# Narrow triangular products and quarters of a dense projection in alternation on TensorE

## The chip, the core and the metric

The kernel runs on one core of a Trainium2 chip. The metric is the device time of one execution in microseconds (us), as the median of several runs. TensorE (PE) multiplies matrices; a product is a weight load (PEld) and a pass of moving columns. VectorE (DVE), ScalarE (ACT) and GpSimd (POOL) do the elementwise work, and SyncE (SP) issues most transfers.

## The reference, cut to what matters

Four layers act on 512 tokens of width 1024: two of a first kind (attention and long convolution) and two of a second kind. The change is in the second kind alone, so it acts twice in an execution. Such a layer holds a gated delta rule (four heads, 128 wide), a latent attention and a gated linear recurrence:

```python
# gated delta rule: a unit triangular system for every chunk and head
a_mat = where(strict, einsum(kbeta, kc) * decay, 0.0) + eye(C)
sol = triangular_solve(a_mat, rhs, lower=True, unit_diagonal=True)
u, w = sol[..., :DV], sol[..., DV:]
_, o = lax.scan(step, state0, xs)          # the state runs over the chunks
o_a = rmsnorm(o, gdn_out_norm) * silu(gz)
...
# linear recurrence
u = causal_dwconv(lx, lru_conv_w) + lru_conv_b
o_c = rg_lru(u, ...) * silu(lz)            # lz = 512 columns of h @ w_in
mixed = concatenate([o_a, o_b, o_c])
return x + mixed @ w_out
```

## The kernel before

Everything is written in Tile, which takes the instructions in the order of the code and gives each engine its own queue in an order that it plans by modelled times: an instruction whose inputs or buffers are not there is passed over, and a later one that is ready is put ahead of it. On the chip each queue then runs in that order. `issue_after(ins)`, used through `self.after`, makes the matmuls traced inside it stand behind `ins` in TensorE's queue.

A dense projection (`projT`) takes one chunk of weights of 128 by 1024 and 24 matmuls of 512 moving columns, three for each of eight blocks of the contraction, since each factor is held as a rounded part and a remainder (`wh`, `wl`). `wchunk` fetches a chunk (line 280), ACT rounds it (line 266), DVE or POOL makes the remainder (line 267). There are two raw buffers (`wr`) and three each of `wh` and `wl`, shared by all projections and taken in the order of the code.

A layer of the second kind (`layer2`) traces, in this order: `mla_pre`; `gdn_front`, which builds the triangular blocks and solves their 32-wide diagonal blocks on DVE (`solve32`, a chain of 62 operations), sends the result to DRAM (line 1396) and fetches it back spread over the partitions (`spread`, lines 1415 and 1417); `lru_open`, three convolution projections; `gdn`, which first has four gate projections for `gz`, then the inverse (`gdn_inv`), then the state recurrence of four steps; `lru`, the linear recurrence in four column blocks c; `mla_v` and `mla`, the attention.

`gdn_inv` joins the 32-wide inverses to 128-wide ones by four sets of narrow products, `p1` (line 1440), `p2` (1446 and 1448), `p3` (1459) and `p4` (1464). Each set has four steps i, each step four heads, and each head one float32 product (two in `p2`), which the trace counts as two instructions with 128 weight columns and 32 or 64 moving columns. A step writes half of a PSUM buffer; ACT copies it out (lines 1442, 1453, 1455, 1460, 1465), and the later sets read the copies. Then `pw` and `pu` (lines 1470 and 1474, 128 moving columns) apply the inverse.

`lru(c)` runs two products with block weights (lines 1228 and 1231), a chain of ACT, DVE and POOL work to a scan, and then the projection of its output gate (24 matmuls with chunk 28 + c), whose `silu2` (lines 701 and 702) goes to a tile `gz` of its own; POOL multiplies it with the scan into `o`. In c = 2 the fourth convolution projection, `conv(3)`, stands ahead of that block's products.

Of the kernel before, what the change touches and what calls it, by code (L numbers as in the profile page):

```python
# [16 lines left out]
ADD, SUB, MUL, MAX = ALU.add, ALU.subtract, ALU.mult, ALU.max  # L17

P = 128
# [149 lines left out]
class Kern:  # L169
# [672 lines left out]
    def gates(self, l, h, ma, mg):  # L842

        ma.append(self.U())
        mg += [self.U(), self.T("mg", (P, 4, S))]
        for f in range(4, 8):
            self.gate(l, h, 32 + f, ma[1][:, f - 4])
            yield
        for f in range(8):
            self.gate(l, h, 40 + f, mg[f // 4][:, f % 4])  # L850
            yield
# [337 lines left out]
    def lru_open(self, l, h):  # L1189

        nc, A = self.nc, self.A
        c2 = self.c2
        bh = self.sm(8, "bh")
        nc.vector.tensor_scalar(bh, c2[:, C2_BR:C2_BR + 8], 0.5, None, op0=MUL)
        sp = self.sm(4, "sp")
        nc.vector.tensor_scalar(sp, c2[:, C2_AP:C2_AP + 4], -1.0, None, op0=MUL)
        sp = self.softplus(sp, 4)
        sp2, ny = self.sm(4, "sp2"), self.sm(4, "ny")
        nc.vector.tensor_scalar(sp2, sp, 2.0, None, op0=MUL)
        nc.vector.tensor_scalar(ny, sp, -4.0, None, op0=MUL)  # L1200
        us = {}

        def conv(c):
            ps = self.ps("acc")
            last = self.projT(self.wchunk(A[f"xin{l}"][24 + c], 8, P), h, ps)
            us[c] = self.T("g2" if c == 2 else "lu")
            self.conv4(us[c], ps, C2_LW + 4 * c, bias=c2[:, C2_LB + c:C2_LB + c + 1])
            return last

        for c in range(3):  # L1210
            last = conv(c)
        return bh, sp2, ny, us, conv, last

    def lru(self, l, h, opened):
        nc, A = self.nc, self.A
        bh, sp2, ny, us, conv, _ = opened
        o = self.U()
        for c in range(4):
            w = self.T("lw", (P, 2, P))
            nc.gpsimd.memset(w, 0.0)  # L1220
            for q in range(2):
                r = slice(64 * q, 64 * q + 64)
                nc.sync.dma_start(w[r, :, r], A[f"lw{l}"][q][:, c])
            if c == 2:
                conv(3)
            u = us[c]
            pr, pi = self.ps("av"), self.ps("av")
            nc.tensor.matmul(pr, w[:, 0], u, start=True, stop=True)
            t, ti, dc = self.T("l"), self.T("g2"), self.T("l")
            nc.scalar.activation(t, pr, AF.Tanh, scale=0.5, bias=bh[:, c:c + 1])  # L1230
            nc.tensor.matmul(pi, w[:, 1], u, start=True, stop=True)
            nc.scalar.activation(ti, pi, AF.Tanh, scale=0.5, bias=bh[:, 4 + c:5 + c])
            nc.vector.scalar_tensor_tensor(u, ti, 1.0, u, op0=ADD, op1=MUL)

            nc.scalar.activation(dc, t, AF.Exp, scale=ny[:, c:c + 1], bias=ny[:, c:c + 1])
            nc.scalar.activation(t, t, AF.Tanh, scale=sp2[:, c:c + 1], bias=sp2[:, c:c + 1])
            nc.scalar.activation(t, t, AF.Sqrt, scale=0.25)
            nc.vector.scalar_tensor_tensor(t, dc, 1.0, t, op0=ADD, op1=MUL)
            nc.gpsimd.tensor_tensor(u, u, t, op=MUL)
            nc.vector.tensor_tensor_scan(t, dc, u, 0.0, op0=MUL, op1=ADD)  # L1240
            ps = self.ps("acc")
            self.projT(self.wchunk(A[f"xin{l}"][28 + c], 8, P), h, ps)
            gz = self.T("l")
            self.silu2(gz, ps)
            nc.gpsimd.tensor_tensor(o[:, c], t, gz, op=MUL)
        return o

    def decays(self, l, gab):
# [172 lines left out]
            nc.vector.transpose(self.diag(XT, k), xc[rs(k)])  # L1421
        return xd, xc, xtc, XT

    def gdn_inv(self, lead, at, t1, X, kb, v2):


        nc = self.nc
        mm = nc.tensor.matmul
        cp = nc.scalar.activation
        xd, xc, xtc, XT = X  # L1430

        def banks(tag, shape):
            ps = [self.ps(tag, (P, 2) + shape) for _ in range(2)]
            return [ps[i // 2][:, i % 2] for i in range(4)]

        p1 = banks("lg", (4, 64))
        for i in range(4):
            with self.after(lead):
                for c in range(4):
                    mm(p1[i][:, c], at[:, i, c], xd[:, 4 * i + c], start=True, stop=True)  # L1440
            for b in (0, 64):
                cp(t1[b + 32:b + 64, i, :, b:b + 32], p1[i][b + 32:b + 64, :, b // 2:b // 2 + 32], AF.Copy)
        p2 = banks("tr", (2, 4, 32))
        for i in range(4):
            for c in range(4):
                mm(p2[i][:, 0, c], XT[:, i, c], t1[:, i, c, 0:32], start=True, stop=True)
            for c in range(4):
                mm(p2[i][:, 1, c], t1[:, i, c], xtc[:, 4 * i + c], start=True, stop=True)

            xi = xd[:, 4 * i:4 * i + 4]  # L1450
            nc.gpsimd.memset(xi[64:96, :, 32:64], 0.0)
            nc.gpsimd.tensor_copy(xi[32:64, :, 32:64], xc[32:64, 4 * i:4 * i + 4])
            cp(xi[32:64, :, 0:32], p2[i][32:64, 0], AF.Copy, scale=-1.0)
            for b in (0, 64):
                cp(XT[b:b + 32, i, :, b + 32:b + 64], p2[i][b:b + 32, 1], AF.Copy, scale=-1.0)
        p3 = banks("lg", (4, 64))
        for i in range(4):
            for c in range(4):
                mm(p3[i][:, c], at[:, i, c], xd[:, 4 * i + c], start=True, stop=True)
            cp(t1[64:128, i, :, 0:64], p3[i][64:128], AF.Copy)  # L1460
        p4 = banks("tr", (4, 64))
        for i in range(4):
            for c in range(4):
                mm(p4[i][:, c], t1[:, i, c], XT[:, i, c, 64:128], start=True, stop=True)
            cp(XT[0:64, i, :, 64:128], p4[i][0:64], AF.Copy, scale=-1.0)
        for i in range(4):
            ts = slice(i * P, (i + 1) * P)
            pw = self.ps("lg", (P, 4, P))
            for c in range(4):
                mm(pw[:, c], kb[:, i, c], XT[:, i, c], start=True, stop=True)  # L1470
            cp(kb[:, i], pw, AF.Copy)
            pu = self.ps("tr", (P, 4, P))
            for c in range(4):
                mm(pu[:, c], XT[:, i, c], v2[:, c, ts], start=True, stop=True)
            cp(v2[:, :, ts], pu, AF.Copy)

    def gdn(self, l, h, lead, q2, k2, v2, at, an, kb, egs, ssq, t1, X):
        nc, A = self.nc, self.A
        mm = nc.tensor.matmul
        gz = self.U()  # L1480
        for c in range(4):
            ps = self.ps("acc")
# [2 lines left out]

        for i in range(4):
            nc.gpsimd.tensor_tensor(at[:, i], at[:, i], self.mbc(self.lv), op=MUL)
        self.gdn_inv(lead, at, t1, X, kb, v2)
        kd, un, wt = k2, v2, kb

        st = [self.T("st", (P, 2, P)) for _ in range(2)]
# [5 lines left out]
        for i in range(4):  # L1497
# [3 lines left out]
            for q in range(2):  # L1501
                hs = slice(2 * q, 2 * q + 2)
                s1 = st[q]
                ps = self.ps("lg", (P, 2, P))
# [15 lines left out]
            o = self.T("go", (P, 4, P))  # L1520
            nc.vector.tensor_tensor(o, po, self.bc(eg[:, 0:4]), op=MUL)
            p2 = self.ps("tr", (P, 4, P))
# [7 lines left out]
            r = self.sm(4, "hr")  # L1530
# [129 lines left out]
```

## Time and profile before

| | us |
|---|---|
| median of three runs | 1890.8 |
| lowest and highest run | 1885.38, 1893.59 |
| profiled execution, its own time | 1893.08 |
| its span in the trace | 1891.3 |
| TensorE busy in the span | 1854.0 (98%) |
| DVE, ACT, POOL busy | 1254.6, 900.1, 659.9 |
| mean granted TensorE clock | 0.992 of full speed |

The span runs from the first to the last instruction, and 1.8 us of the execution's time lie around it. Times below are from the span's start. A matmul's listed duration is that of its passage; matmuls overlap, and what one costs in a row is the distance from its start to the next one's start.

### The profile page before, as it was taken

To read this page: it belongs to the slowest core of one execution; us is meant where nothing else is said; L and a number is where in the kernel's file an instruction comes from. 1 tells how busy PE (TensorE), PEld (TensorE's weight loads), DVE (VectorE), ACT (ScalarE), POOL (GpSimd) and SP (SyncE) were. 2 spreads that over 40 slices of the span, in tenths; PEclk is the share of its full clock that TensorE was granted. 3 is DMA by queue.
4 is the path that set the end of the run, shared out by engine and by line. 5 is a ranking of instruction groups with operands and counts; after the bars stand their busy time and mean duration, and the time that the engine had idled before them with its cause. 6 is when DMAs were issued, how large, how long until landed. Compare 5 with 4: busy or idle time off the path is not lost.

```text
span 1891.3 us, 26054 instructions
## 1 busy us (share of the span) xinstructions
PE 1854.0 (98%) x9604; PEld 1560.9 (83%) x9604; DVE 1254.6 (66%) x2238; ACT 900.1 (48%) x1761; POOL 659.9 (35%) x566
## 2 busy tenths in 40 slices
PE   8999999999999999999999999999999999999998
PEld 5878888887788788888888888888888888888886
DVE  6898688664788849775567954757235895465722
ACT  4766432334476542223455356656325535665631
POOL 2455343443245535443146332111114643311110
PEclk9999999999999999999999989999999998999999
DMA  5333433324323353233332321213343222121242
GB/s 178 98 120 110 145 112 107 112 89 164 116 96 106 105 160 108 100 101 123 128 105 70 97 73 30 69 59 115 101 136 101 79 84 79 36 69 59 77 131 90
DMA packets 75656, 190.84 MB, mean 101 GB/s; under 512 B 15714, under 2 KB 25698, under 8 KB 75528
## 3 DMA queue, kind: packets, MB, share of 16 engines
q1 hardware_dynamic: 69448, 184.71, 30.1%
q0 software_dynamic: 1696, 3.41, 0.7%
q10 hardware_dynamic: 4384, 1.05, 0.3%
q8 instruction: 76, 1.25, 0.3%
q14 instruction: 52, 0.43, 0.1%
HBM read 171.29 MB, written 17.84 MB: 100 GB/s over the span
## 4 chain that ended last, share of the span: by engine, by line
PE 75%; DVE 13%; issue 4%; ACT 3%; POOL 3%; DMA 2%; ACTq 0%; SPq 0%; DVEq 0%; POOLq 0%
PE acc L258 13%; PE acc L260 13%; PE acc L259 13%; PE fl L259 5%; PE fl L258 5%; PE fl L260 5%; PE av L1181 2%; DVE wl L267 2%; DVE g L1005 1%; PE av L259 1%; PE av L258 1%; PE av L260 1%; PE av L588 1%; PE lg L259 1%; PE lg L260 1%
## 5 line engine op out<-in xcount | busy, mean ns | idle before, releaser
L266 ACT ACTIVATE wh<-wr 128x1024 fp32r<-128x1024 f32 (+3 forms) x268 | 256.0, 955 | 448.3 <-PE acc L259 160.9
L258 PE MATMUL acc<-u,wh 128*128 128x512 f32 x996 | 397.1, 399 | 0.2
L259 PE MATMUL acc<-u,wh 128*128 128x512 f32 x996 | 393.2, 395 | 0.0
L260 PE MATMUL acc<-u,wl 128*128 128x512 f32 x996 | 392.5, 394 | 0.0
L267 POOL TENSOR_TENSOR wl<-wr,wh 128x1024 fp32r<-128x1024 f32 (+3 forms) x86 | 186.2, 2165 | 490.1 <-ACT wh L266 451.0
L267 DVE TENSOR_TENSOR wl<-wr,wh 128x1024 fp32r<-128x1024 f32 (+3 forms) x182 | 217.5, 1195 | 170.0 <-ACT wh L266 159.6
L258 PEld LDWEIGHTS acc<-u,wh 128*128 128x128 f32 x996 | 187.2, 188 | 42.7 <-issue 3.7
L260 PEld LDWEIGHTS acc<-u,wl 128*128 128x128 f32 x996 | 187.2, 188 | 39.5 <-issue 2.6
L259 PEld LDWEIGHTS acc<-u,wh 128*128 128x128 f32 x996 | 187.3, 188 | 38.3 <-issue 2.9
L259 PE MATMUL fl<-u,wh 128*128 128x512 f32 x316 | 128.6, 407 | 0.0
L260 PE MATMUL fl<-u,wl 128*128 128x512 f32 x316 | 126.5, 400 | 0.0
L258 PE MATMUL fl<-u,wh 128*128 128x512 f32 x316 | 125.9, 398 | 0.0
L260 PE MATMUL acc<-wh,u 128*128 128x512 f32 (+1 forms) x212 | 79.5, 375 | 0.3
L258 PE MATMUL acc<-wh,u 128*128 128x512 f32 (+1 forms) x212 | 78.2, 376 | 1.6 <-DVE l L702 1.2
L259 PE MATMUL acc<-wl,u 128*128 128x512 f32 (+1 forms) x212 | 78.7, 371 | 0.0
L260 PEld LDWEIGHTS fl<-u,wl 128*128 128x128 f32 x316 | 60.3, 191 | 14.9 <-issue 3.0
L259 PEld LDWEIGHTS fl<-u,wh 128*128 128x128 f32 x316 | 60.3, 191 | 13.3 <-issue 2.0
L258 PEld LDWEIGHTS fl<-u,wh 128*128 128x128 f32 x316 | 60.1, 190 | 13.2 <-issue 1.5
L677 ACT ACTIVATE p<-p,mx 128x512 f32<-128x512 f32 x64 | 45.7, 715 | 37.4 <-DVE mx L675 37.4
L790 POOL TENSOR_TENSOR w<-w,ab 128x256 f32<-128x256 f32 x32 | 37.7, 1179 | 69.2 <-DVE w L789 64.0
L321 ACT ACTIVATE sq<-x 128x512 f32<-128x512 f32 x40 | 25.2, 631 | 68.6 <-DVE x L1613 38.2
L1168 ACT ACTIVATE p<-p,amx 128x128 f32<-128x128 f32 (+1 forms) x64 | 35.8, 560 | 28.2 <-DVE amx L1167 27.5
(636 smaller groups left out, 4438.7 us busy)
## 6 DMA issues: line engine op xcount, KB each, us to landing
wr<-in_win SPq DMA_DIRECT2D x88, 512.0 KB, 3.5
wr<-in_xin SPq DMA_DIRECT2D x64, 512.0 KB, 3.4
wr<-in_xout SPq DMA_DIRECT2D x32, 512.0 KB, 3.5
hd<-f SPq DMA_DIRECT2D x32, 256.0 KB, 4.2
hs<-hd SPq DMA_DIRECT2D x32, 256.0 KB, 2.8
wr<-in_wout SPq DMA_DIRECT2D x16, 512.0 KB, 3.4
xd<-x SPq DMA_DIRECT2D x12, 512.0 KB, 3.1
x<-xd SPq DMA_DIRECT2D x12, 512.0 KB, 4.8
```

The costliest lines, as they stand in the source:

```text
L258: mm(ps, l[0], r[0], start=first, stop=False)
L259: mm(ps, l[0], r[1], start=False, stop=False)
L260: return mm(ps, l[1], r[0], start=False, stop=last)
L266: nc.scalar.activation(hi, src, AF.Copy)
L267: (nc.gpsimd if pool else nc.vector).tensor_tensor(lo, src, hi.bitcast(F32), op=SUB)
L321: self.nc.scalar.activation(self.T("sq"), self.xt(i)[:, h * S:(h + 1) * S], AF.Square, scale=1.0 / math.sqrt(D), accum_out=self.ms2[i][:, ...
L588: nc.tensor.matmul(po[:, i], wt[:, kt], v[:, kt, hd * P:(hd + 1) * P], start=kt == 0, stop=kt == 3)
L677: nc.scalar.activation(pp[c], pp[c], AF.Exp, bias=mx[:, c:c + 1], accum_out=s0[:, i:i + 1] if c == 0 else s)
L790: nc.gpsimd.tensor_tensor(a[:, 0], a[:, 0], b[:, 1], op=ADD)
L1005: nc.vector.scalar_tensor_tensor(y[:, d:], ps[:, :S - d], w(n), y[:, d:], op0=MUL, op1=ADD)
L1168: nc.scalar.activation(p[:, :n], p[:, :n], AF.Exp, bias=mx, scale=scale, accum_out=s)
L1181: mm(po[:, ts], v[hd // 4][:, k, (hd % 4) * P:(hd % 4 + 1) * P], w[:, k], start=k == 0, stop=k == i)
```

## The change

The four output gate projections of the linear recurrence move from `lru` into the inverse. `lru_open` now returns a generator, `gates()`, that traces them in order, with a halt after every second of the eight blocks of the contraction, that is after six matmuls. So there are 16 quarters. `gdn_inv` takes the steps of `p1` to `p4` and the quarters in turn: step, quarter, step, quarter, 16 times; each stands behind the one before in TensorE's queue by `issue_after`. The first step stands behind the third convolution projection, as before. The gate's `silu2` writes to `o[:, c]`, and the scan is multiplied into it in place, so that the separate tile for the gate is gone. `o` is allocated with the first quarter. `pw`, `pu` and the state recurrence are as they were.

```diff
+        def gates():
+            o.append(self.U())
+            for c in range(4):
+                ps = self.ps("acc")
+                hi, lo = self.wchunk(A[f"xin{l}"][28 + c], 8, P)
+                for k in range(8):
+                    last = self.mm3(ps, (hi[:, k], lo[:, k]), h[k], k == 0, k == 7)
+                    if k == 7:
+                        self.silu2(o[0][:, c], ps)
+                    if k % 2:
+                        yield last
...
-        return bh, sp2, ny, us, conv, last
+        return bh, sp2, ny, us, conv, o, (last, gates())
...
-            ps = self.ps("acc")
-            self.projT(self.wchunk(A[f"xin{l}"][28 + c], 8, P), h, ps)
-            gz = self.T("l")
-            self.silu2(gz, ps)
-            nc.gpsimd.tensor_tensor(o[:, c], t, gz, op=MUL)
+            nc.gpsimd.tensor_tensor(o[:, c], t, o[:, c], op=MUL)
...
+        def turn(products):
+            nonlocal last
+            for each in (products, lambda: next(other)):
+                with self.after(last):
+                    last = each()
+
+        def four(p, left, right):
+            for c in range(4):
+                r = mm(p[:, c], left(c), right(c), start=True, stop=True)
+            return r
...
         for i in range(4):
-            with self.after(lead):
-                for c in range(4):
-                    mm(p1[i][:, c], at[:, i, c], xd[:, 4 * i + c], start=True, stop=True)
+            turn(lambda: four(p1[i], lambda c: at[:, i, c], lambda c: xd[:, 4 * i + c]))
...
-            for c in range(4):
-                mm(p2[i][:, 0, c], XT[:, i, c], t1[:, i, c, 0:32], start=True, stop=True)
-            for c in range(4):
-                mm(p2[i][:, 1, c], t1[:, i, c], xtc[:, 4 * i + c], start=True, stop=True)
+            def both():
+                four(p2[i][:, 0], lambda c: XT[:, i, c], lambda c: t1[:, i, c, 0:32])
+                return four(p2[i][:, 1], lambda c: t1[:, i, c], lambda c: xtc[:, 4 * i + c])
+
+            turn(both)
...
-            for c in range(4):
-                mm(p3[i][:, c], at[:, i, c], xd[:, 4 * i + c], start=True, stop=True)
+            turn(lambda: four(p3[i], lambda c: at[:, i, c], lambda c: xd[:, 4 * i + c]))
...
-            for c in range(4):
-                mm(p4[i][:, c], t1[:, i, c], XT[:, i, c, 64:128], start=True, stop=True)
+            turn(lambda: four(p4[i], lambda c: t1[:, i, c], lambda c: XT[:, i, c, 64:128]))
```

## Rows read from the trace of the kernel before

**Rows 1.** The page: busy us (share of the span) and instructions of each engine.

```profile
PE 1854.0 (98%) x9604; PEld 1560.9 (83%) x9604; DVE 1254.6 (66%) x2238; ACT 900.1 (48%) x1761; POOL 659.9 (35%) x566
```

**Rows 2.** TensorE's waits over the span: us in total, times, longest.

```profile
PE ft L349 <- DVE xn L342: 7.5, 1, 7.5
PE lg L667 <- DVE mx L671: 5.1, 3, 2.1
...
PE acc L258 <- DVE l L702: 1.2, 1, 1.2
```

**Rows 3.** Stretches: us, then busy us (instructions) by engine, PEclk, DMA share, GB/s.

```profile
1109.00:1114.50 5.50, 5.50 (x51) 5.46 (x49) 3.61 (x4) 1.88 (x7) 3.45 (x8) 0.99 0.31 75
1114.50:1117.90 3.40, 3.40 (x8) 2.06 (x8) 0.00 (x0) 2.14 (x5) 0.40 (x2) 0.51 0.32 123
1117.90:1121.30 3.40, 3.40 (x33) 3.40 (x31) 0.76 (x2) 3.35 (x6) 0.00 (x0) 0.99 0.00 0
1121.30:1128.10 6.80, 6.80 (x25) 5.48 (x25) 0.98 (x2) 4.25 (x10) 0.32 (x1) 0.50 0.00 0
...
1588.60:1595.50 6.90, 6.90 (x25) 5.50 (x25) 0.14 (x1) 2.96 (x8) 2.23 (x5) 0.52 0.20 78
...
1598.90:1605.70 6.80, 6.80 (x26) 5.48 (x26) 0.99 (x2) 4.23 (x10) 0.32 (x1) 0.51 0.00 0
```

**Rows 4.** TensorE in order of time, third layer: start, us, line, operands, count.

```profile
1092.05 1.02 PE L1228 MATMUL av<-lu,lw 128*128 128x512 f32 x2
...
1098.38 1.02 PE L1231 MATMUL av<-lu,lw 128*128 128x512 f32 x2
...
1102.88 0.39 PE L259 MATMUL acc<-u,wh 128*128 128x512 f32 x1
1103.11 0.39 PE L260 MATMUL acc<-u,wl 128*128 128x512 f32 x1
1103.56 1.97 PE L1440 MATMUL lg<-xd,at 128*128 128x64 f32 x16
...
1109.10 1.90 PE L1440 MATMUL lg<-xd,at 128*128 128x64 f32 x16
1110.83 1.03 PE L1446 MATMUL ft<-X,XT 128*128 128x32 f32 x8
...
1122.37 2.80 PE L1459 MATMUL lg<-xd,at 128*128 128x64 f32 x12
1124.96 2.02 PE L1231 MATMUL av<-lu,lw 128*128 128x512 f32 x2
...
1145.14 1.06 PE L1470 MATMUL lg<-XT,kb 128*128 128x128 f32 x8
1145.96 0.48 PE L258 MATMUL acc<-u,wh 128*128 128x512 f32 x1
1146.27 0.40 PE L259 MATMUL acc<-u,wh 128*128 128x512 f32 x1
```

**Rows 5.** TensorE's groups between 1092 and 1103.5 us, one of three alike.

```profile
L258 PE MATMUL acc<-u,wh 128*128 128x512 f32 x14 | 6.3, 447 | 0.0
```

**Rows 6.** POOL in order of time; in brackets the idle time before, and its releaser.

```profile
1096.90 0.66 POOL L1396 DMA_DIRECT2D dm<-u  x1 [12.18 <-DVE u L1395]
...
1100.21 1.39 POOL L1415 DMA_DIRECT2D xd<-dm  x2 [1.98 <-DMA dm<-u]
```

**Rows 7.** ACT in order of time: roundings of weight chunks, and a copy of `p1`.

```profile
1092.02 1.06 ACT L266 ACTIVATE wh<-wr 128x1024 fp32r<-128x1024 f32 x1 [3.90 <-DVE st L1393]
...
1098.39 1.06 ACT L266 ACTIVATE wh<-wr 128x1024 fp32r<-128x1024 f32 x1 [0.61 <-POOL st L1516]
...
1104.67 0.55 ACT L1442 ACTIVATE X<-lg 32x128 f32<-32x128 f32 x2 [2.73 <-PE lg L1440]
...
1106.78 1.06 ACT L266 ACTIVATE wh<-wr 128x1024 fp32r<-128x1024 f32 x1 [0.66 <-PE acc L259]
```

**Rows 8.** TensorE in order of time, fourth layer.

```profile
1579.66 1.97 PE L1440 MATMUL lg<-xd,at 128*128 128x64 f32 x16
```

More of the change, by code (lines that the diff above doesn't have):

```diff
@@ L1208, in conv @@
             return last
+        o = []
+        def gates():
[9 more added lines that the diff above has]
+                        yield last
         for c in range(3):
             last = conv(c)
-        return bh, sp2, ny, us, conv, last
+        return bh, sp2, ny, us, conv, o, (last, gates())
     def lru(self, l, h, opened):
         nc, A = self.nc, self.A
-        bh, sp2, ny, us, conv, _ = opened
-        o = self.U()
+        bh, sp2, ny, us, conv, (o,), _ = opened
         for c in range(4):
@@ L1422, in spread, with gdn_inv @@
         return xd, xc, xtc, XT
-    def gdn_inv(self, lead, at, t1, X, kb, v2):
+    def gdn_inv(self, last, other, at, t1, X, kb, v2):
         nc = self.nc
@@ L1487, in gdn @@
             nc.gpsimd.tensor_tensor(at[:, i], at[:, i], self.mbc(self.lv), op=MUL)
-        self.gdn_inv(lead, at, t1, X, kb, v2)
+        self.gdn_inv(*lead, at, t1, X, kb, v2)
         kd, un, wt = k2, v2, kb
```

## The prediction

> **What bounds the kernel now.** I read the page first: TensorE is busy for 1854.0 of 1891.3 us, and no other engine comes above 66% [rows 1]. The view of TensorE's waits over the whole span says the same from the other side: the largest is 7.5 us ahead of the first work, then 5.1 us in three parts of at most 2.1 us; of the lines that the change touches there is one, 1.2 us for a gate's `silu2` [rows 2]. So the time is TensorE's work plus its few waits, and a projection that is moved changes nothing unless TensorE stands still for it, or runs at another clock.
>
> The stretches by granted clock come next. Behind 1109 us of the third layer 51 instructions, nearly all narrow, run in a row, and from 1114.5 the clock is at about half, its lower level of 1.2 GHz, for 3.4 us; after another run of narrow products it is at half for 6.8 us. The fourth layer has 6.9 and 6.8 us [rows 3]. Between 1122.37 and 1124.96, at half, 12 narrow instructions cost 0.216 us each; between 1109.10 and 1110.83, at full, 16 cost 0.108 us each [rows 4]. That is what the narrow sets cost now.
>
> Then TensorE in order of time ahead of the first narrow product, which the reader should look at longest. From 1092.05, the first `lru` pair, to 1103.56, the first `p1`, there are 11.5 us, and TensorE is not idle in them [rows 4]. They hold the two `lru` pairs and 42 wide matmuls in three groups of 14, all into `acc` from `wh` and `wl` [rows 5]. By the order of the code these are output gates: all of block 0 (24) and 18 of block 1. The last projection of `gz` ends where they begin.
>
> Why does `p1` start at 1103.56? POOL has waited 12.18 us for the last operation of `solve32` when it sends the result at 1096.90; it waits 1.98 us more for its landing and fetches `xd` at 1100.21 [rows 6]. `p1` multiplies `xd`. So a chain of DVE work and two transfers sets the start of the inverse, and the gates were what TensorE did meanwhile.
>
> **What the change adds: a wait.** `turn` puts the first quarter behind the first step of `p1` in TensorE's queue, and every later quarter behind that. The 42 wide matmuls can't run before `xd` lands any more. One costs 0.23 us (1102.88 to 1103.11) [rows 4], so 42 x 0.23 = 9.7 us in which TensorE has nothing, unless something else is put there. In the fourth layer the first `p1` likewise opens a run of 16 at 1579.66 [rows 8], behind the same code, so I count it twice: 19.3 us.
>
> What could fill it? `pw`, `pu` and the state recurrence need the inverse. The `lru` pair of block 0 is there already. The next candidate is `conv(3)`, 24 wide matmuls. But weight buffers are three, taken in the order of the code, and gate chunks 0 to 2 now come before it. A rounding starts when an older chunk's matmuls are through: at 1092.02, at 1098.39 and at 1106.78, the last two each some 0.2 us behind the end of a projection and the last released by PE [rows 7]. With no gate running, no buffer comes free, so `conv(3)`, and behind it the chunks of `mla_v` and `mla`, stay out until the fourth quarter is done. Bounds: nothing if all is filled, 19.3 us if nothing is; I take 19.3.
>
> **What the wait does to the clock.** With 10 us almost without products, I expect half rate at the first steps. The four stretches at half lasted 3.4 to 6.9 us [rows 3] and lose half of that, 1.7 to 3.4 us; I take 2.5 for each layer, 5.1 in all. The lower bound is nothing. The Trainium skill, "TensorE: Matmul & The Clock Gate", section "HAM oscillation — how this bites in real kernels", has the rule that speaks against this change: a wait for data between bursts of matmuls puts the engine back to half rate, so that the next burst begins cold. By it the sum is the one below; without it, 5.1 us less. No row here shows such a wait in mid-kernel, as the longest was 2.1 us.
>
> **What it removes.** The falls: 3.4 + 6.8 + 6.9 + 6.8 = 23.9 us at half in which TensorE was busy throughout [rows 3], so 12.0 us at most. In the new order no more than 16 narrow instructions (a step of `p2`, 1.7 us) stand between six wide ones (1.4 us). A run of 16 at 1103.56 was followed by no fall; the fall came in the long run behind 1109.10 [rows 3, 4]. I take all 12.0. The 1.2 us for `silu2` [rows 2] goes too, as that gate is now done long before; its bounds are 0 and 1.2.
>
> **The turns themselves.** Eight narrow instructions ahead of a wide one take 0.82 us, and the wide one 0.31 instead of 0.23 us (1145.14, 1145.96, 1146.27) [rows 4]: 0.90 us against 8 x 0.108 = 0.87 us in a run. That is 1 us for 32 turns at most, and the mixed order of before paid part of it: nothing. A step that reuses a PSUM buffer waits for the copy: 0.55 us for `p1`, begun 0.24 us behind its product [rows 4, 7]; the quarter of 1.4 us covers that, unless ACT is in a rounding of 1.06 us or a chain of `lru`. I take 0.7 us a layer, 1.4 in all, between 0 and 3 a layer.
>
> **What costs nothing.** The gates' `silu2`, chunk fetches and POOL multiplications are as many as before. SP's queue has `conv(3)`'s chunk behind four gate chunks; nothing but `lru(3)` waits for it, whose result is wanted at the layer's end. The 42 matmuls move past the first product, and the inverse takes about as many more wide ones, so the recurrence keeps most of its cover; if it lost that, the price would show as waits behind `L1506` and `L1513`.
>
> **The sum.** 19.3 + 5.1 + 1.4 - 12.0 - 1.2 = +12.6 us on the profiled execution's 1893.1 gives 1905.7. That execution lies 2.3 us above the median of the runs, so I forecast 1903 for a median. Its own range, by the bounds of the clock (3.4 to 6.8), of the copies (0 to 6) and of the 1.2: 1900 to 1911.
>
> **Rivals.**
>
> *The wait is filled.* Place: 1092 to 1103 us and its twin. If `xd` landed when `gz` ends, or other wide work were queued there, only the gains stay: 1893.1 - 12.0 - 1.2 + 1.4 = 1881.3, less 2.3 is 1879: faster. If only `conv(3)` gets in (24 x 0.23 = 5.5 us a layer), 1892. It decides once 12.6 of the 24.4 us of wait and cold clock are gone. For it: the planner takes anything ready. Against it: three buffers, three gate chunks. Chance 0.17: 0.07 for the whole, 0.10 for a part.
>
> *The clock stays up through the wait.* The two `lru` products of block 0 stand in it. With no copy waits either, the sum is 5.1 + 1.4 lower: 1897. Chance 0.10.
>
> *The half rate returns in the turns,* or the mixture does not lift it. For it: the `p2` steps, with 32 moving columns, do little for the 1.7 us that they take, and every rise seen so far came with wide products in a row. As many falls as before would give back 12.0: 1915. Chance 0.13.
>
> **How the numbers follow.** The forecast has 0.60. Runs of this kernel spread over 0.4%, so 0.5% is about what a measurement can tell from no change: 1881 to 1900. Faster is the wholly filled wait, 0.07. Within are the partly filled one, the clock that stays, and some 0.08 of the forecast's low end: 0.28. Slower: 0.65. The range for 8 in 10 runs from 1888, which takes in the partly filled wait, to 1917, which takes in the returned falls.
>
> **What would show it.** Right: a wait of 8 to 10 us ahead of `L1440` in both layers, the largest that TensorE has; half rate at the first steps; full rate from the second or third step on; chunk roundings that stop between 1092 and some 1110 us. Wrong: wide matmuls between the last of `gz` and `L1440`; half rate around `L1446`; or a wait ahead of each of the second and fourth steps, which would mean that copies pace the turns.

## The result and the profile after

The changed kernel takes 1907.88 us (median of five runs, 1907.35 to 1909.35) against 1890.8 us before: slower, with a ratio of 1.0095 (95% interval 1.0071 to 1.0118). The median lies 17 us higher, and the two profiled spans are 16.3 us apart (1907.5 and 1891.3). The forecast was 1903 us, within 1888 to 1917.

The page of the kernel after, engine line, as in [rows 1]:

```profile
PE 1853.2 (97%) x9604; PEld 1559.3 (82%) x9604; DVE 1245.8 (65%) x2238; ACT 898.8 (47%) x1761; POOL 659.7 (35%) x566
```

TensorE has the same 9604 instructions and is busy for as long; what is new is time in which it does nothing. Its waits over the whole span, to be set beside [rows 2] (L1242 and L1245 are the two `lru` products, L1228 and L1231 before; L1456 is the helper `four`, now the line of all narrow products of `p1` to `p4`):

```profile
PE av L1242 <- DMA lw<-in_lw: 14.6, 2, 7.5
...
PE lg L667 <- DVE mx L671: 4.3, 2, 2.2
...
PE av L1245 <- ACT l L1244: 2.5, 3, 1.1
...
PE tr L1456 <- ACT XT L1477: 1.6, 1, 1.6
PE lg L1456 <- ACT X L1481: 1.6, 2, 1.0
...
PE ft L1456 <- ACT XT L1477: 0.4, 1, 0.4
```

The largest is new: 14.6 us in two parts, one for each layer of the second kind. With two of the 1.1 us parts of `L1245` it makes 16.8 us ahead of the first narrow product. The 1.2 us for a gate's `silu2` (L702) is gone. All waits of this list together are 46.6 us, against 28.4 us before.

TensorE in order of time, third layer, the answer to [rows 4]:

```profile
1092.63 1.02 PE L1242 MATMUL av<-lu,lw 128*128 128x512 f32 x2
1094.77 1.13 PE L1245 MATMUL av<-lu,lw 128*128 128x512 f32 x2 [1.11 <-ACT l L1244]
1103.34 2.04 PE L1242 MATMUL av<-lu,lw 128*128 128x512 f32 x2 [7.45 <-DMA lw<-in_lw]
1105.18 1.80 PE L1456 MATMUL lg<-xd,at 128*128 128x64 f32 x8
1106.75 0.77 PE L258 MATMUL acc<-u,wh 128*128 128x512 f32 x1
...
1108.84 1.02 PE L1245 MATMUL av<-lu,lw 128*128 128x512 f32 x2
1109.70 1.00 PE L1456 MATMUL lg<-xd,at 128*128 128x64 f32 x8
```

Between 1092.63 and 1103.34 stand block 0's two `lru` products, each a pair of instructions, and nothing else; the 42 wide matmuls that stood there before [rows 5] come behind the first `p1` at 1105.18. The second pair L1242 belongs to block 1 of the linear recurrence. Before, it came later; now the planner, with nothing else ready, put it ahead of `p1`, and its own small weights (`lw`) end the wait. The first `p1` then costs 1.57 us for eight instructions (1105.18 to 1106.75), and the second 0.81 (1109.70 to 1110.51, where the next wide one starts): half rate, then full.

The stretches of the kernel after, to be read beside [rows 3]:

```profile
1097.80:1103.30 5.50, 0.00 (x0) 0.00 (x0) 2.33 (x4) 2.39 (x3) 3.71 (x7) 0.50 0.68 179
1103.30:1107.90 4.60, 4.56 (x13) 3.36 (x14) 2.48 (x4) 1.23 (x3) 3.21 (x6) 0.50 0.24 61
1107.90:1112.00 4.10, 4.10 (x22) 3.16 (x21) 2.96 (x4) 1.91 (x4) 0.91 (x3) 0.98 0.04 8
1131.80:1135.20 3.40, 3.40 (x13) 2.83 (x12) 0.78 (x1) 1.52 (x4) 0.00 (x0) 0.52 0.00 0
585.70:589.10 3.40, 3.40 (x9) 2.67 (x9) 3.40 (x7) 2.80 (x6) 1.80 (x3) 0.52 0.00 0
...
1585.90:1590.00 4.10, 0.00 (x0) 0.00 (x0) 1.25 (x3) 1.32 (x2) 2.36 (x5) 0.51 0.76 214
1590.00:1596.10 6.10, 6.01 (x16) 4.47 (x17) 3.34 (x5) 1.23 (x3) 3.52 (x6) 0.50 0.22 53
```

The clock falls in the wait and stays at its lower level, 1.2 GHz, for 4.6 us of work in the third layer and 6.1 us in the fourth. From 1108 us on it is full through the alternation (1.00 from 1112 to 1131.8 and from 1135.2 to 1165), but for one stretch at 1131.8 behind a copy wait; in the fourth layer it is 1.00 from 1596.1 to 1660. The long falls of before are gone.

The roundings of weight chunks on ACT (to [rows 7]) halt as expected:

```profile
1092.59 1.06 ACT L266 ACTIVATE wh<-wr 128x1024 fp32r<-128x1024 f32 x1 [3.90 <-DVE st L1403]
...
1119.55 1.05 ACT L266 ACTIVATE wh<-wr 128x1024 fp32r<-128x1024 f32 x1
```

None for 27 us: three gate chunks hold all buffers until the first gate is through.

### The profile page after: what moved, and what is told of

It is laid out like the page before. It is cut to its first block, busy times and chain, and to the rows that moved or that the text cites. A ratio compares the mean times of both kernels' runs of the same rounds, so it can differ in the third digit from the quotient of the medians.

```text
span 1907.5 us, 26057 instructions
## 1 busy us (share of the span) xinstructions
PE 1853.2 (97%) x9604; PEld 1559.3 (82%) x9604; DVE 1245.8 (65%) x2238; ACT 898.8 (47%) x1761; POOL 659.7 (35%) x566
## 4 chain that ended last, share of the span: by engine, by line
PE 70%; DVE 16%; issue 4%; ACT 3%; POOL 3%; DMA 3%; ACTq 0%; SPq 0%; POOLq 0%; DVEq 0%
PE acc L258 12%; PE acc L260 12%; PE acc L259 12%; PE fl L258 5%; PE fl L259 5%; PE fl L260 5%; DVE wl L267 2%; PE av L1181 2%; DVE g L1005 1%; DVE st L1403 1%; PE av L258 1%; PE av L259 1%; PE av L260 1%; DMA wr<-in_wout 1%; PE lg L260 1%
```

## The experiments

Theory W is the prediction's: the loss is TensorE's wait ahead of the first step, made by tying every quarter behind it, with half rate behind the wait; the falls that are gone pay part of it back. The rival T is that the turns themselves cost: a strict order, paced by ACT's copies and the chain of the linear recurrence. All runs were compared with the kernel before on the same chip.

**Seven quarters ahead** (`e1_seven_ahead`). The 42 wide matmuls go back into the wait; nine quarters keep their turns, and the last seven steps have none.

```diff
+        for _ in range(7):
+            with self.after(last):
+                last = next(other)
...
-            for each in (products, lambda: next(other)):
+            for each in (products, lambda: next(other, last)):
```

> Seven quarters (the 42 wide matmuls that filled the wait before) are queued ahead of the first narrow step, the other nine keep their turns. Theory W, the loss is the wait ahead of the first step: the two waits of 7 to 9 us per layer go and the clock does not fall in them, so 17 us of wait and some 4.6 us of cold clock come back; with the falls of before still gone, about 1907.9 - 21 = 1886 to 1888 us. Theory T, the turns are what costs (copies and the linear recurrence's chain on ACT pace a strict order): nine of the sixteen turns remain, so more than half of the loss does, 1900 us or more.

Measured: 1887.79 us, ratio to before 0.998 (0.9959 to 1.0001). All of the 17 us lost came back, as W expected. TensorE in order of time in this kernel:

```profile
1100.60 0.39 PE L258 MATMUL acc<-u,wh 128*128 128x512 f32 x1
1101.29 1.02 PE L1242 MATMUL av<-lu,lw 128*128 128x512 f32 x2
1103.29 1.08 PE L1456 MATMUL lg<-xd,at 128*128 128x64 f32 x8 [0.97 <-DMA xd<-dm]
1104.17 0.48 PE L258 MATMUL acc<-u,wh 128*128 128x512 f32 x1
```

The wait ahead of the first step is 0.97 us, and that step takes 0.88 us. The first quarter's six wide matmuls take 1.47 us (1104.17 to 1105.64, where the next product starts) against 2.09 us in the changed kernel (1106.75 to 1108.84). The granted clock is 1.00 in both inverses (1103.2 to 1130 and 1572 to 1600 us). T asked for 1900 us or more and fell.

**No ties** (`e2_no_order`). The trace order stays in alternation, the ties go.

```diff
-            nonlocal last
-            for each in (products, lambda: next(other)):
-                with self.after(last):
-                    last = each()
+            with self.after(last):
+                products()
+            next(other)
```

> Steps and quarters are traced in the same alternation, but no quarter or step is tied behind another; only the lead on the third convolution projection stays. W: the planner fills the wait with gates again, the waits go; whether the falls come back depends on what is left for the narrow steps, so between 1883 (no falls) and 1893 us (as many falls as before, 12 us at half lost). T: also near 1890. What it tells apart is the gain: if the clock falls return here, the tie is what kept the clock up; if not, the alternation in the trace order was enough.

Measured: 1894.35 us, ratio 1.0014 (0.9997 to 1.0032): the kernel before again. The planner puts the gates into the wait, and the narrow products run together as before. The stretches of its profiled execution, which at 1885.55 us was the lowest of its twelve runs:

```profile
1107.00:1128.00 21.00, 21.00 (x159) 19.83 (x158) 2.98 (x4) 8.10 (x24) 0.96 (x4) 1.00 0.18 60
1584.80:1588.20 3.40, 3.40 (x13) 2.92 (x13) 0.00 (x0) 0.80 (x3) 0.00 (x0) 0.51 0.01 2
1591.60:1598.40 6.80, 6.80 (x27) 6.22 (x27) 0.00 (x0) 1.56 (x5) 0.00 (x0) 0.51 0.10 28
```

The fourth layer has 10.2 us at half; the third none, with as long a run of narrow products. So the order in which the code names them does not keep the clock up; the ties do, and without them, in this execution, the fall comes in one layer and not in the other. Its mean granted clock, 0.996, is the highest of the twelve; the others have 0.990 to 0.994, so more time at half.

**Steps in the order 0, 2, 1, 3** (`e3_steps_0213`). In each of the four sets, so that successive steps write different PSUM buffers.

```diff
-        for i in range(4):
+        for i in (0, 2, 1, 3):
```

> The four steps of each set run as 0, 2, 1, 3, so that successive steps write different PSUM buffers and none waits for the copies of the step just before it; the ties and the quarters stay. W: only the copy waits go (3.5 us in the changed kernel's trace) and perhaps one fall that stood behind the longest of them (1.7 us): 1903 to 1905 us. T: the turns were the loss, so most of the 17 us comes back: below 1895 us.

Measured: 1903.3 us, ratio 1.0061 (1.0039 to 1.0082), 4.6 us below the changed kernel. No wait of L1456 for ACT is left among its listed waits, the fall at 1131.8 is gone, and the waits ahead of the inverse are as they were:

```profile
PE av L1242 <- DMA lw<-in_lw: 14.2, 2, 7.2
...
PE av L1245 <- ACT l L1244: 2.2, 2, 1.1
```

So T has a share, in this test about a quarter of the loss.

**Filler in the wait** (`e4_filler`). It adds 36 products of the activations with themselves, which nothing reads.

```diff
+        ps, hh = self.ps("acc"), h[0][0]
+        for n in range(36):
+            with self.after(last):
+                last = mm(ps, hh[:, 0:P], hh, start=n == 0, stop=n == 35)
```

> 36 wide matmuls that belong to nothing (a product of the activations with themselves, never read) are queued behind the last projection of the recurrence's gate and ahead of the first step; all else is as in the changed kernel. The wait is as long as before, but TensorE works through it. W with a clock that falls in the wait: the first steps run at full rate, 2.3 us a layer come back, 1903 us; the granted clock is 1.0 from 1092 us on. If the half rate behind the wait cost nothing, 1908 us.

Measured: 1915.55 us, ratio 1.0132 (1.0103 to 1.016), 7.7 us above the changed kernel: a miss. TensorE in order of time shows why it doesn't isolate the clock:

```profile
1094.87 8.33 PE L1511 MATMUL acc<-u 128*128 128x512 f32 x36
1103.03 1.02 PE L1242 MATMUL av<-lu,lw 128*128 128x512 f32 x2
1106.33 1.08 PE L1456 MATMUL lg<-xd,at 128*128 128x64 f32 x8 [2.27 <-DMA xd<-dm]
```

Its longer copy waits, and a stretch of its clock:

```profile
PE lg L1456 <- ACT X L1481: 4.4, 2, 2.2
...
PE ft L1456 <- ACT XT L1477: 2.5, 2, 1.5
```

```profile
1108.10:1111.50 3.40, 3.40 (x10) 2.14 (x9) 3.05 (x5) 3.35 (x4) 0.32 (x1) 0.52 0.00 0
```

The filler went ahead of block 0's `lru` products, which had used the wait; they and block 1's pair now come behind it, and a wait of 2.27 us for `xd` remains. Filler and that wait for `xd` are 21.2 us over both layers (2 x 8.2 + 4.8) against 16.8 us of waits in the changed kernel, and the copy waits are 6.9 us against 3.6. The clock was expected at 1.0 from 1092 us on. It is full through the filler and the wait for `xd`, and at half for 3.4 us from 1108.1, some 2 us after that wait, and again from 1626.9. Set against the changed kernel, 4.4 us of filler and wait, 3.3 of copies and 3.4 of falls (three of 3.4 us, one of them at 787, where the other has the one at 1131.8), less 5.3 of half rate that is gone, make 5.8 us, and the spans (1913.3 and 1907.5) are 5.8 apart. That sum was made afterwards: it fits the price of the cold clock, but no run isolates it.

**Four quarters ahead** (`e6_four_ahead`), the first kernel's edit with `range(4)`.

> Four quarters (one whole gate, 24 wide matmuls, 5.5 us) ahead of the first step, twelve in the turns. W: of the wait of 8.6 us a layer some 3 stay, so 11 us come back, and the clock falls later or not at all (0 to 4.6 us): 1893 to 1897 us. T: thirteen-sixteenths of the turns stay as they are, so about 1905.

Measured: 1897.59 us, ratio 1.0032 (1.002 to 1.0044), 0.6 us above the range of W and far from T's 1905. Its waits, then its stretches by clock:

```profile
PE lg L1456 <- DMA xd<-dm: 10.1, 2, 5.1
```

```profile
1100.00:1105.10 5.10, 0.11 (x1) 0.00 (x0) 0.69 (x1) 2.15 (x4) 3.29 (x6) 0.98 0.63 178
1105.10:1111.80 6.70, 6.66 (x20) 5.08 (x20) 2.69 (x4) 4.58 (x7) 3.72 (x6) 0.51 0.36 108
```

The wait is 5 us a layer, not 3, as the second product of block 0 and block 1's first no longer run in it. It is ended by `xd`, as the prediction's chain has it. With none, four and seven quarters ahead the waits there are 16.8, 10.1 and 1.9 us, and the medians 1907.88, 1897.59 and 1887.79: the time goes with the wait. In the kernel with four the clock is still full as the wait ends and at half in the 6.7 us of work behind it.

**The fourth convolution ahead** (`e8_conv3_ahead`). All 16 quarters keep their turns; other wide work is traced before the gate of `gz`.

```diff
-            us[c] = self.T("g2" if c == 2 else "lu")
+            us[c] = self.T("g2" if c >= 2 else "lu")
...
-        for c in range(3):
+        for c in range(4):
             last = conv(c)
...
-            if c == 2:
-                conv(3)
```

> All 16 quarters keep their turns behind the first step; the fourth convolution projection (24 wide matmuls) moves from the recurrence's third block to the other three, ahead of the gate of gz, so that its weights are no longer behind four gate chunks. W with the step on the weight buffers: any wide work that may run before the first step shortens the wait, by 5.5 us a layer; 1893 to 1898 us. If the wait had another cause than missing wide work, it would only start later and stay as long: 1908 us.

Measured: 1899.1 us, ratio 1.0046 (1.0029 to 1.0064), 8.8 us below the changed kernel and 1.1 us above the range of W. The waits ahead of the inverse are 11.6 us for `xd` and 2.3 us for the second `lru` product (L1243 here, L1245 in the changed kernel); `L1454` is the helper `four`:

```profile
PE lg L1454 <- DMA xd<-dm: 11.6, 2, 5.8
...
PE av L1243 <- ACT l L1242: 2.3, 2, 1.2
```

So 10.9 us of wide work went in, and the waits shrank by 2.9 us only (13.9 against 16.8). One reason is that block 1's pair no longer gets into the wait. The other is that the wait ends later. POOL, first in the changed kernel, then in this one:

```profile
1100.81 1.39 POOL L1425 DMA_DIRECT2D xd<-dm  x2 [1.76 <-DMA dm<-u]
```

```profile
1104.06 1.39 POOL L1423 DMA_DIRECT2D xd<-dm  x2 [2.77 <-DMA dm<-u]
```

DVE now does the convolution of `conv(3)` (three operations of 0.73 us from 1082.85 on) among the operations of `solve32`; POOL waits 14.74 us for their last instead of 12.17, and `xd` is fetched 3.25 us later. Of the 7.5 us between the spans (1907.5 and 1900.0), 2.9 are the waits; 3.6 are the copy waits, of which this kernel lists none, and 1.7 the fall at 1131.8, which it does not have; the half rate behind the wait cost some 0.8 more (6.5 and 5.9 us of work). Why the copies no longer wait was not followed. So wide work that is let in need not be a gate, but it shortened the wait much less than the expectation had it, and the gain of 8.8 us is mostly not the wait's.

**Seven ahead and the steps 0, 2, 1, 3** (`e5_seven_0213`), both edits together.

> Seven quarters ahead and the steps in the order 0, 2, 1, 3. W: the 1.6 us of copy waits that the kernel with seven quarters ahead still had in its trace go as well; no fall in the inverse. About 3 us under that kernel: 1883 to 1886 us, and faster than the kernel before by some 0.4%. T would expect the copies to have been most of the cost, and a far lower time than that, under 1880.

Measured: 1882.26 us (1880.23 to 1884.02), ratio 0.9957 (0.9939 to 0.9974): the fastest version, some 10 us below the median of the kernel before, and 0.7 us below the range of W. T's time under 1880 did not come. The stretches around both inverses are at full clock throughout:

```profile
1103.00:1125.00 22.00, 21.03 (x134) 18.07 (x132) 9.78 (x12) 13.96 (x28) 10.22 (x16) 1.00 0.25 76
1125.00:1150.00 25.00, 25.00 (x162) 21.73 (x162) 5.90 (x8) 18.02 (x30) 5.48 (x4) 1.00 0.10 27
1570.00:1595.00 25.00, 23.81 (x142) 20.14 (x141) 12.14 (x15) 14.82 (x27) 13.21 (x20) 1.00 0.37 101
```

## Why the prediction was right

The mechanism held in the main. The wait appeared where it was put; it went as the gates were put back into it (e6, e1), and its end depends on the landing of `xd` (seen in e1, e6 and e8). The roundings halted for 27 us, as they should if three gate chunks kept `conv(3)` out; no run changed the number of buffers, so this step rests on the halt. The gain of the kernel that lets `conv(3)` in does not prove it, as most of that gain lies elsewhere. In the inverse the falls went where ties hold, but for one of 3.4 us in the changed kernel and two in the one with the filler, and came back without the ties in one layer of the profiled execution.

The terms of the sum, against the two profiled spans:

| term | forecast, us | measured, us |
|---|---|---|
| wait ahead of the first step | +19.3 | +16.8 |
| half rate behind it | +5.1 | +5.3 (half of 4.6 and 6.1) |
| copies in the turns | +1.4 | +3.6 (1.6 + 1.6 + 0.4) |
| falls | -12.0 | -10.3 (one of 3.4 us at 1131.8 left) |
| `silu2` | -1.2 | -1.2 |
| elsewhere: two falls of 3.4 us in the first layers, at 585.7 and 636.8 | none | +3.4 |
| sum | +12.6 | +17.6, measured 16.3 |

Of the rest of 1.3 us, 1.0 is in other, smaller waits: all together rose by 18.2 us, where the terms above make 19.2 (that of L667 alone fell from 5.1 to 4.3). The last 0.3 us was not traced.

That 1903 came so near to 1907.88 is partly luck. The wait was forecast 2.5 us too long and the copies 2.2 us too short, which nearly cancels, and most of what the sum lacks, 3.4 of 3.7 us, came from layers that the change does not touch.

Two terms were mis-sized. The wait was shorter because block 1's `lru` pair came forward into its end; I had held only block 0's for possible. The pair ran from 1103.34 to 1105.18, and `xd` landed at about 1104.2 (an estimate: its second transfer begins at 1101.5 and takes 2.6 to 2.7 us to land), so without the pair some 0.9 us more of that wait would show. The copies cost more: I let the quarter of 1.4 us cover a copy, unless ACT is in a rounding. ACT in order of time shows what came between:

```profile
1126.50 0.82 ACT L1250 ACTIVATE l<-l,sp 128x512 f32<-128x512 f32 x1
1127.33 1.28 ACT L1251 ACT_TABLE_LOAD   x1
1128.62 0.63 ACT L1251 ACTIVATE l<-l 128x512 f32<-128x512 f32 x1
1129.28 0.27 ACT L1475 ACTIVATE xd<-tr 32x128 f32<-32x128 f32 x1
1129.56 0.55 ACT L1477 ACTIVATE XT<-tr 32x128 f32<-32x128 f32 x2
```

A piece of the recurrence's chain, with a table load, holds ACT from 1126.50 to 1129.28; the copies of a `p2` step stand behind it, the next step waits 1.6 us for them, and the clock falls for 3.4 us. With the steps as 0, 2, 1, 3 this goes, and 4.6 us come back. One reading was loose: the roundings at 1098.39 and 1106.78 [rows 7] stand 0.2 us behind the start of a projection's last matmul (1098.14 and 1106.58), not behind its end; no term hangs on it.

On the clock, the Trainium skill, "TensorE: Matmul & The Clock Gate", section "HAM oscillation — how this bites in real kernels", holds that a burst behind a long wait begins cold. The runs agree: behind the waits of 7.45 and 5.03 us the first 4.6 and 6.7 us of work ran at half rate; behind 0.97 us they did not.

## What to carry to other kernels

When work is tied into an alternation, look at what that work covered where it stood: here 42 dense products hid a chain of DVE work and two transfers, and tying the first of them behind the chain's result opened the wait. Give the alternation only what is left after that cover is paid for; here seven quarters ahead and nine in the turns. Work that is put into the wait must not delay the chain that ends it, as the fourth convolution did on DVE. And let successive steps write different buffers, so that a strict order doesn't also wait for copies.

## What the runs showed of the hardware that was not expected

A wait that is the same in two executions need not have the same effect on the clock. In a layer of the first kind, ahead of line 667 at some 585 us, TensorE waits 2.12 us in both kernels. First the kernel before, then the kernel after, TensorE in order of time:

```profile
586.16 0.51 PE L667 MATMUL lg<-qk,qk 128*128 128x512 f32 x1 [2.12 <-DVE mx L671]
...
586.74 0.40 PE L258 MATMUL acc<-u,wh 128*128 128x512 f32 x1
586.97 0.40 PE L259 MATMUL acc<-u,wh 128*128 128x512 f32 x1
```

```profile
585.47 0.51 PE L667 MATMUL lg<-qk,qk 128*128 128x512 f32 x1 [2.12 <-DVE mx L671]
...
586.21 0.63 PE L258 MATMUL acc<-u,wh 128*128 128x512 f32 x1
586.63 0.63 PE L259 MATMUL acc<-u,wh 128*128 128x512 f32 x1
```

One goes on at 0.23 us for a wide product, the other at 0.43 us, for 3.4 us. The layers of the first kind are the same in all kernels here, and this wait is 2.11 to 2.13 us in all nine profiled executions: six have the fall behind it, three (the kernel before, the untied one and the one with steps 0, 2, 1, 3) have none. The prediction's longest wait in mid-kernel, 2.1 us, had no fall behind it; that was one execution. The untied kernel says the same of narrow products: a long run of them was followed by a fall in one layer and not in the other. What decides between the two was not tried.

Time at half rate goes with the spread of the kernel before over 25 runs, 1881 to 1902 us. The mean granted clock of every run is on record: 0.998 in the two fastest (1881.11 and 1881.72 us), 0.988 in the two slowest (1901.07 and 1902.06). As an estimate, 0.010 less of 1890 us is 38 us more at half, of which half, 19 us, is lost; the measured distance is 19 to 21 us. One run of the kernel with seven quarters ahead (1891.39 us at 0.946) does not fit this sum. The fastest version ran at 0.997 to 0.999 in all eight of its executions, in 1880 to 1884 us, where the kernel before is only in its fastest ones: its gain looks like that of the falls that it no longer has.
